# The modulation stage of a hybrid attention and Fourier layer: order of loads, the split of one matrix product between TensorE and VectorE, and the first tile's rows

## The chip, the cores and the metric

The kernel runs on one core of one Trainium2 chip. The metric is the device time of one launch in microseconds (us). Each comparison runs the kernels on the same chip.

## The reference

One layer of a diffusion backbone, in float32, for 256 context tokens (`x_prompt`) and 2048 latent tokens (`x_sample`), 1024 channels. Both streams share all weights.

```
m = silu(cvec) @ w_mod + b_mod              # cvec: c for latent, c_ctx for context tokens; w_mod 1024 x 6144
sh1, sc1, g1, sh2, sc2, g2 = split(m, 6)
h = rms_norm(x, norm1_g) * (1 + sc1) + sh1
q, k, v, f = split(h @ w_in)                # 1024 x 2048: four groups of 512 columns
mix = concat(diff_attention(q, k, v), fourier(f)) @ w_out
x = x + g1 * mix
h = rms_norm(x, norm2_g) * (1 + sc2) + sh2
x = x + g2 * (relu(h @ w1) ** 2 @ w2)
```

The change concerns the way from the inputs to the first rows of `h` and of `h @ w_in`. For these, columns 0 to 2047 of `w_mod` (the shift `sh1` and the scale `sc1`, for both condition vectors) are needed first.

## The kernel before

The tokens are 18 tiles of 128 rows; tiles 0 and 1 are context. The kernel has stages: modulation and projection of all tiles (to about 450 us), Fourier mixing, attention, output projection, MLP. Products with large matrices are made in three passes (`mm3`, L87 to L90): each operand is split into a high half in a shortened float format (`h`, a cast) and the low half that remains (`l`, a subtraction), and high by high, high by low and low by high are summed in PSUM. ScalarE makes the high half, VectorE the low half.

The part at hand (L437 to L549) stands in a `manual_schedule` block: each engine's queue has the order in which the code is written. The loop over tiles 1 to 16 behind it (L552 ff.) is ordered by the scheduler of the framework, which places each instruction by a timeline of its own from the start of the program on; the last tile and the later stages are written out by hand again. Inputs are loaded through SP's queue (`nc.sync`), some small ones through ACT's (`nc.scalar`) and POOL's (`nc.gpsimd`).

In order, the part at hand does this:

- `setup_small` (L92) loads the condition vectors, `b_mod` and the norm gains as rows of one tile, applies SiLU to the two vectors (ScalarE's Exp, VectorE's reciprocal), transposes the tile on TensorE and copies it to `cols`: one column per 128 channels.
- `load(0)` loads tile 0, then eight tiles `wm` of W_mod follow (128 rows x 2048 columns, 1 MB each); `load(1)` stands behind the third.
- `norm` (L204) for tile 0: ScalarE squares and sums, VectorE takes the mean, POOL raises to the power -1/2 (`pow_mhalf`, L85), VectorE scales the rows. TensorE then transposes tile 0 (L451).
- Per W_mod tile, TensorE multiplies three blocks of 512 columns by the two condition columns (L455, in float32: each block is two instructions in the trace), and VectorE multiplies and adds the last 512 columns by one condition value per partition, for both conditions (`macc`, L459 and L461). Behind the fifth stands the `norm` of tile 1.
- W_in is loaded in 16 halves of 512 KB (`w_half`, `win`): six at once, each later one as soon as a half before it has been split.
- `mod_cols` (L480): the sums of two rows are copied out and transposed into columns (L484); VectorE's 512 sums are reduced over partitions by matmuls with a column of ones (L489). Bias and gains make `modc` and `scale1` (L492, L201, L202). `load_gains` (L111) then issues six small loads on POOL's queue, each broadcasting a row of 64 values to 128 partitions.
- Tile 0's transposed rows are modulated (`h_mod`, four on ScalarE and four on VectorE, L500 and L502), and both 512-column parts are split (L510, L511). Tile 1 is transposed (L515).
- For each of eight row blocks `k` of W_in: four high halves on ScalarE (L523), four low halves on VectorE (L524), and TensorE's twelve matmuls of tile 0 with groups 0 to 3, into four PSUM banks `pj`. In between stand tile 1's modulation (blocks 1 to 4), its split (block 5) and the `norm` of tile 2 (block 6).
- `f_post(0)` empties the bank of group 3 (L402); `proj(1, 0)`, the first projection of tile 1, takes that bank.

Of the kernel before, what the change touches and what calls it, by code (L numbers as in the profile page):

```python
# [37 lines left out]
def f32(ap):  # L38
    return ap.bitcast(F32)


def body(tc, a, out):
    nc = tc.nc
    ctx = ExitStack()
    with ctx:
# [43 lines left out]
            nc.tensor.matmul(ps, lh, rl, start=False, stop=False)  # L89
            nc.tensor.matmul(ps, ll, rh, start=False, stop=last)  # L90

        def setup_small(pool, pps):  # L92
# [3 lines left out]
            nc.sync.dma_start(rows[8:16, :], a["c_ctx"].rearrange("(r p) -> r p", p=P))  # L96
            nc.sync.dma_start(rows[32:80, :], a["b_mod"].rearrange("o (r p) -> (o r) p", p=P))
            nc.scalar.dma_start(rows[80:88, :], a["norm1_g"].rearrange("o (r p) -> (o r) p", p=P))
            nc.scalar.dma_start(rows[88:96, :], a["norm2_g"].rearrange("o (r p) -> (o r) p", p=P))
            nc.scalar.dma_start(rows[96:97, :], a["subln_g"])  # L100
            e = pool.tile([16, P], F32, tag="t2", name="e", bufs=6)
# [67 lines left out]

        FIN = {}  # L170

        def mod_sums(t2, pps, sums, gi):

            z = t2(f"quad{gi}")[:, 0:224]
            nc.gpsimd.memset(z, 0.0)
            nc.gpsimd.tensor_add(z[:, 96:128], ident[:, 0:32], ident[:, 32:64])
            for q in (2, 3):
                nc.gpsimd.tensor_add(z[:, 96:128], z[:, 96:128], ident[:, 32 * q:32 * q + 32])
            FIN[gi] = pm = pps.tile([P, 4, 2, 4], F32, tag="pm", name=f"pm{gi}")
            for q in range(4):  # L180
                nc.tensor.matmul(pm, z[:, 96 - 32 * q:224 - 32 * q], sums[:, :, :, q::4], start=(q == 0), stop=(q == 3))
# [48 lines left out]
        with ExitStack() as c1:  # L230
# [6 lines left out]
            def t2(nm):  # L237
                return p1.tile([P, 512], F32, tag="t2", name=nm, bufs=6)
# [197 lines left out]
            wsrc = a["w_in"][0].rearrange("(k p) n -> p k n", p=P)  # L436
            with tc.manual_schedule():  # L437
                with tc.tile_pool(name="p0r", bufs=3) as rows, tc.tile_pool(name="p0m", bufs=KD - 3, side="right") as more:
                    setup_small(p1, pps)
                    load(0)  # L440
                    wm = []
                    for k in range(KD):
                        wm.append((rows if k < 3 else more).tile([P, 2048], F32, tag="row", name=f"wm{k}"))
                        nc.sync.dma_start(wm[k], wmod[:, k, 0:2048])
                        if k == 2:
                            load(1)
                    norm(p1, X[0], "a0")
                    pr = [pp.tile([P, 512], F32, tag="pj", name=f"pr{gi}", bufs=4) for gi in range(4)]
                    pt0 = [pp.tile([P, 4, P], F32, tag="pt", name=f"pta0_{b}") for b in range(2)]
                    for k in range(KD):  # L450
                        nc.tensor.transpose(pt0[k // 4][:, k % 4, :], X[0][:, k * P:(k + 1) * P], ident)  # L451
                    acc = [t2(f"macc3_{s}") for s in range(2)]
                    for k in range(KD):
                        for gi in range(3):
                            nc.tensor.matmul(pr[gi][0:2, :], cols[:, k:k + 9:8], wm[k][:, gi * 512:gi * 512 + 512], start=(k == 0), stop=(k == KD - 1))  # L455
                        for s in range(2):
                            wk, sc = wm[k][:, 1536:2048], cols[:, 8 * s + k:8 * s + k + 1]
                            if k == 0:
                                nc.vector.tensor_scalar_mul(acc[s], wk, sc)  # L459
                            else:  # L460
                                nc.vector.scalar_tensor_tensor(acc[s], wk, sc, acc[s], op0=ALU.mult, op1=ALU.add)  # L461
# [6 lines left out]
                with tc.tile_pool(name="p0h", bufs=6, reuse_waits="tile") as halves:  # L468
# [4 lines left out]
                        wraw.append(halves.tile([P, 1024], F32, tag="half", name=f"win{k}_{h}"))  # L473
                        nc.sync.dma_start(wraw[n], wsrc[:, k, h * 1024:h * 1024 + 1024])

                    for n in range(6):
                        w_half(n)
                    pm = pps.tile([P, 16, 2], F32, tag="pg", name="pm16")

                    def mod_cols(gi):  # L480
                        r = t2(f"mr{gi}")
                        (nc.vector.tensor_copy if gi == 1 else nc.scalar.copy)(r[0:2, :], pr[gi][0:2, :])
                        for j in range(4):
                            nc.tensor.transpose(pm[:, gi * 4 + j, :], r[0:2, j * P:(j + 1) * P], ident[0:2, 0:2])  # L484

                    mod_cols(0)
                    for s in range(2):
                        for j in range(4):
                            nc.tensor.matmul(pm[:, 12 + j, s:s + 1], acc[s][:, j * P:(j + 1) * P], ones, start=True, stop=True)  # L489
                    mod_cols(2)  # L490
                    mod_cols(1)
                    nc.vector.tensor_add(modc[:, 0:16, :], pm, cols[:, 32:48].unsqueeze(2).to_broadcast([P, 16, 2]))  # L492
# [4 lines left out]
                    def h_mod(dst, pt, k, eng):  # L497
                        sc, sh = scale1[:, k, 1:2], modc[:, k, 1:2]
                        if eng is nc.vector:
                            nc.vector.tensor_scalar(dst, pt[:, k % 4, :], sc, sh, op0=ALU.mult, op1=ALU.add)  # L500
                        else:
                            nc.scalar.activation(dst, pt[:, k % 4, :], AF.Identity, bias=sh, scale=sc)  # L502

                    h0 = [t2(f"hTa0_{b}").rearrange("p (k t) -> p k t", k=4) for b in range(2)]
                    for k in range(4):
                        h_mod(h0[0][:, k, :], pt0[0], k, nc.scalar)
                        h_mod(h0[1][:, k, :], pt0[1], 4 + k, nc.vector)
                    for b in range(2):
                        hi, lo = (x[:, b * 4:b * 4 + 4, :] for x in HH[0])
                        nc.vector.tensor_copy(hi, h0[b])  # L510
                        nc.vector.tensor_sub(lo, h0[b], f32(hi))  # L511
                    X.pop(0)
                    pt1 = [pp.tile([P, 4, P], F32, tag="pt", name=f"pta1_{b}") for b in range(2)]
                    for k in range(KD):
                        nc.tensor.transpose(pt1[k // 4][:, k % 4, :], X[1][:, k * P:(k + 1) * P], ident)  # L515
                    X.pop(1)
                    PJ.update({(0, g): pp.tile([P, 512], F32, tag="pj", name=f"pj0_{g}", bufs=4) for g in (3, 2, 0, 1)})
                    hT = p1.tile([P, KD, P], F32, tag="hT", name="hTa1", bufs=1)
                    load(2)
                    for k in range(KD):  # L520
                        for g in range(4):
                            w = wraw[2 * k + g // 2][:, g % 2 * 512:g % 2 * 512 + 512]
                            nc.scalar.copy(wh[g][k], w)  # L523
                            nc.vector.tensor_sub(wl[g][k], w, f32(wh[g][k]))  # L524
                            if g % 2 and 2 * k + g // 2 + 6 < 16:
                                w_half(2 * k + g // 2 + 6)
                        if 1 <= k < 5:
                            for x in (2 * k - 2, 2 * k - 1):
                                h_mod(hT[:, x, :], pt1[x // 4], x, nc.scalar)
                        if k == 5:  # L530
                            nc.scalar.copy(HH[1][0], hT)
                            nc.vector.tensor_sub(HH[1][1], hT, f32(HH[1][0]))
                        if k == 6:
                            norm(p1, X[2], "a2")
                        for g in range(4):
                            mm3(PJ[0, g], HH[0][0][:, k, :], HH[0][1][:, k, :], wh[g][k], wl[g][k], k == 0, k == KD - 1)
                po = c1.enter_context(tc.tile_pool(name="p1o", bufs=2, reuse_waits="tile"))
                f_post(0)
                vo0 = v_out(0)
# [1530 lines left out]
```

## Time and profile before

| | |
|---|---|
| median of 3 runs | 2885.6 us (2884.66 to 2887.24) |
| the profiled run: its time, its span | 2886.51 us, 2884.7 us |
| granted TensorE clock, mean | 0.998 |
| TensorE (PE) busy | 2847.6 us, 99% |
| VectorE (DVE) busy | 2011.5 us, 70% |
| ScalarE (ACT) busy | 1547.0 us, 54% |
| GpSimd (POOL) busy | 1061.7 us, 37% |
| DMA | 492.93 MB, mean 171 GB/s |

A timeline row has start, duration, engine, line, operation, output and inputs, the count of instructions merged into it and, in brackets, how long the engine was idle before it and what released it. The length of a matmul's row contains its way through the array; one follows the other at shorter distances. Starts and names ending in "q" belong to the issuing queue. A row of busy time by stretch has the stretch, its length, the busy time of PE, PEld (weight loads), DVE, ACT and POOL with the number of instructions, the granted TensorE clock, the share of the DMA engines' time, and GB/s.

### The profile page before, as it was taken

How to read it: one execution, taken by the hardware profiler on the slowest of the kernel's cores; microseconds unless marked ns; L12 is line 12 of the kernel's file. 1: busy time of each engine (PE TensorE's matmuls, PEld its weight loads, DVE VectorE, ACT ScalarE, POOL GpSimd, SP SyncE). 2: the span in 40 equal slices, each digit the busy share in tenths (PEclk: the TensorE clock that was granted, in tenths of full speed). 3: DMA queues.
4: the chain of work that ended last, by engine and by line, in shares of the span. 5: the costliest groups of instructions: out<-in, count | busy, mean ns of one | idle time of the engine just before them, and what ended most of it. 6: DMA issues, size and time to landing. Idle time of an engine off the chain costs nothing.

```text
span 2884.7 us, 43207 instructions
## 1 busy us (share of the span) xinstructions
PE 2847.6 (99%) x15119; PEld 2468.6 (86%) x15119; DVE 2011.5 (70%) x3375; ACT 1547.0 (54%) x3503; POOL 1061.7 (37%) x869
## 2 busy tenths in 40 slices
PE   8999999999999999999999999999999999999999
PEld 4888787688888888888889999999998888888887
DVE  6676776898988989865477777778775353345554
ACT  4333322798998989853356565556554332232221
POOL 1112112699999999942223333333332000000000
PEclk9999999999999999999999999999999999999999
DMA  7777888521211312037777677667747464345663
GB/s 283 202 201 190 227 210 231 195 106 43 73 69 45 114 38 98 21 112 208 236 219 233 219 247 229 220 218 238 232 166 254 146 201 137 133 143 185 200 206 110
DMA packets 392779, 492.93 MB, mean 171 GB/s; under 512 B 26467, under 2 KB 306384, under 8 KB 389490
## 3 DMA queue, kind: packets, MB, share of 16 engines
q1 hardware_dynamic: 387136, 479.73, 52.7%
q0 software_dynamic: 1872, 7.28, 0.7%
q10 hardware_dynamic: 3554, 3.17, 0.4%
q8 instruction: 119, 1.95, 0.3%
q14 instruction: 98, 0.80, 0.1%
HBM read 312.58 MB, written 179.59 MB: 171 GB/s over the span
## 4 chain that ended last, share of the span: by engine, by line
PE 91%; DVE 3%; ACT 3%; DMA 2%; issue 1%; POOL 0%; SPq 0%; ACTq 0%; DVEq 0%; POOLq 0%
PE Ss L1022 10%; PE ps L88 8%; PE ps L89 8%; PE ps L90 8%; PE pts L1077 5%; PE po L90 4%; PE po L88 4%; PE po L89 4%; PE pj L88 4%; PE pj L89 4%; PE pj L90 4%; PE pA L1685 2%; PE pA L1686 2%; PE pB L1685 2%; PE pB L1686 2%; PE pB L1687 2%
## 5 line engine op out<-in xcount | busy, mean ns | idle before, releaser
L1027 DVE TENSOR_REDUCE mxs<-Ss 128x1 f32<-128x512 f32 x636 | 413.3, 685 | 63.1 <-PE Ss L1022 52.0
L1362 DVE TENSOR_TENSOR sl<-sr,sh 128x768 fp32r<-128x768 f32 x168 | 161.7, 964 | 337.8 <-ACT sh L1361 337.3
L1062 POOL TENSOR_TENSOR P0s<-P0s,P1s 128x1024 f32<-128x1024 f32 (+2 forms) x128 | 378.7, 2958 | 10.7
L1361 ACT CAST sh<-sr 128x768 fp32r<-128x768 f32 x168 | 140.2, 836 | 424.8 <-PE ps L89 424.8
L1727 POOL TENSOR_TENSOR gs<-g,g 128x384 f32<-128x384 f32 x48 | 69.6, 1451 | 469.8 <-ACT g L1697 410.8
L1046 ACT ACTIVATE P1s<-Ss,mxs 128x512 f32<-128x512 f32 x318 | 215.2, 694 | 36.1 <-DVE mxs L1030 36.1
L88 PE MATMUL pj<-wh,hh 128*128 128x512 f32 x576 | 229.4, 398 | 3.9 <-DVE qn L289 3.2
L89 PE MATMUL ps<-tlT,sh 128*128 128x512 f32 x585 | 229.3, 392 | 0.0
L88 PE MATMUL ps<-thT,sh 128*128 128x512 f32 x585 | 229.0, 391 | 0.0
L89 PE MATMUL pj<-wl,hh 128*128 128x512 f32 x576 | 228.5, 397 | 0.5 <-DVE wl L524 0.5
L90 PE MATMUL ps<-thT,sl 128*128 128x512 f32 x585 | 227.7, 389 | 0.0
L90 PE MATMUL pj<-wh,hl 128*128 128x512 f32 x576 | 227.3, 395 | 0.0
L1046 ACT ACTIVATE P0s<-Ss,mxs 128x512 f32<-128x512 f32 x318 | 214.1, 691 | 5.5 <-DVE mxs L1030 4.9
L1022 PE MATMUL Ss<-KS1s,Qs 128*128 128x512 f32 x636 | 196.2, 420 | 6.2 <-ACT P0s L1046 3.5
L1022 PE MATMUL Ss<-KS0s,Qs 128*128 128x512 f32 x636 | 195.5, 420 | 2.4 <-ACT P1s L1046 2.4
L1077 PEld LDWEIGHTS pts<-ident,P0s 128*128 128x128 f32 x1280 | 157.7, 140 | 42.8 <-issue 2.1
L1077 PE MATMUL pts<-ident,P0s 128*128 128x128 f32 x1280 | 190.5, 272 | 0.7 <-ACT P1s L1046 0.7
L1696 ACT ACTIVATE g<-uz 128x384 f32<-128x384 f32 x144 | 75.8, 527 | 201.0 <-DVE uz L1719 171.3
L1061 POOL TENSOR_SCALAR P1s<-P1s,tots 128x1024 f32<-128x1024 f32 (+2 forms) x128 | 171.7, 1342 | 5.8
L1089 DVE TENSOR_TENSOR als<-pts,ahs 128x512 fp32r<-128x512 f32 x256 | 165.9, 681 | 6.8 <-ACT ahs L1084 6.6
L88 PE MATMUL ps<-ophT,sh 128*128 128x512 f32 x423 | 165.7, 392 | 1.1 <-DVE uz L1719 1.1
L90 PE MATMUL ps<-ophT,sl 128*128 128x512 f32 x423 | 165.7, 392 | 0.0
(531 smaller groups left out, 8056.3 us busy)
## 6 DMA issues: line engine op xcount, KB each, us to landing
sr<-sd SPq DMA_DIRECT2D x84, 768.0 KB
a<-in_w SPq DMA_DIRECT2D x184, 256.0 KB
sd<-gs SPq DMA_DIRECT2D x192, 192.0 KB
sd<-g SPq DMA_DIRECT2D x144, 192.0 KB
wm<-in_w_mod SPq DMA_DIRECT2D x32, 512.0 KB
Qs<-qd SPq DMA_DIRECT2D x32, 512.0 KB
b<-in_w SPq DMA_DIRECT2D x64, 256.0 KB
b<-tsum SPq DMA_DIRECT2D x64, 256.0 KB
```

Source lines behind the costliest of these rows:

```text
L88: nc.tensor.matmul(ps, lh, rh, start=first, stop=False)
L89: nc.tensor.matmul(ps, lh, rl, start=False, stop=False)
L90: nc.tensor.matmul(ps, ll, rh, start=False, stop=last)
L1022: nc.tensor.matmul(S[:, :w], self.Q[:, x, m, j * P:j * P + P], self.hd.KS[m][:, b * 512:b * 512 + w], start=(x == 0), stop=(x == 1))
L1027: nc.vector.tensor_reduce(self.mx[j][:, m, b:b + 1], self.S[j, m, b], axis=AX.X, op=ALU.max)
L1046: nc.scalar.activation(dst, S, AF.Exp, bias=self.mx[j][:, m, 6:7], accum_out=self.sm[j][:, m, b:b + 1])
L1061: nc.gpsimd.tensor_scalar(p, p, tot[:, 3:4], 0.0, op0=ALU.mult, op1=ALU.add)
L1062: nc.gpsimd.tensor_add(d, d, p)
L1077: nc.tensor.transpose(pt[:, c:c + P], self.p0[j][:, (kb + t) * P:(kb + t + 1) * P], ident)
L1089: nc.vector.tensor_sub(t, self.pt[kb], f32(self.A[kb][0]))
L1361: nc.scalar.copy(hi, src)
L1362: nc.vector.tensor_sub(lo, src, f32(hi))
```

## The change

`setup_small` becomes `load_cond`, which only issues the small loads (`c_ctx` now on ACT's queue, `norm1_g` on SP's), and `setup_cond`, which computes and comes after the loads of W_mod. Tile 0 is loaded behind the second W_mod tile, tile 1 behind the second half of W_in, tile 2 (`load(2)`) in row block 1.

VectorE sums 768 of the 2048 columns, TensorE 1280 (512 + 512 + 256). VectorE's sums are reduced by a transposing reduction and four small products with the matrix `quad`, as later modulation groups do. Tile 0's norm stands behind the third W_mod tile, its transposes in pairs behind the fourth to seventh.

The four high halves of row block 0 stand ahead of the scales on ScalarE, the first low half ahead of them on VectorE. Tile 0's rows are made in two parts: channels 0 to 511 (two activations each on ScalarE and VectorE) ahead of the row blocks, the others behind the splits of block 1, where tile 1's norm now stands too. Tile 1's transposes stand behind TensorE's blocks 2 and 4, its modulation in blocks 3 to 6, its split in block 7. Block 7's matmuls go through the groups in the order 3, 2, 0, 1.

```
+        def load_cond(pool):
             rows = pool.tile([P, P], F32, tag="t2", name="rows", bufs=6)
...
-            nc.sync.dma_start(rows[8:16, :], a["c_ctx"]...)
+            nc.scalar.dma_start(rows[8:16, :], a["c_ctx"]...)
-            nc.scalar.dma_start(rows[80:88, :], a["norm1_g"]...)
+            nc.sync.dma_start(rows[80:88, :], a["norm1_g"]...)
...
-                    setup_small(p1, pps)
-                    load(0)
+                    rw = load_cond(p1)
...
-                        if k == 2:
-                            load(1)
-                    norm(p1, X[0], "a0")
+                        if k == 1:
+                            load(0)
+                    setup_cond(p1, pps, rw)
+                    z = quads(t2, "quad0")
+                    pr = [pp.tile([P, 512], F32, tag="pj", name=f"pr{gi}", bufs=4) for gi in range(3)]
...
+                    def at0(k):
+                        return pt0[k // 2 % 2][:, k // 4 * 2 + k % 2, :]
...
                     for k in range(KD):
-                        for gi in range(3):
+                        for gi, w in enumerate((512, 512, 256)):
...
-                            wk, sc = wm[k][:, 1536:2048], ...
+                            wk, sc = wm[k][:, 1280:2048], ...
...
-                        if k == 4:
-                            norm(p1, X[1], "a1")
+                        if k == 2:
+                            norm(p1, X[0], "a0")
+                        if 3 <= k < 7:
+                            for x in (2 * k - 6, 2 * k - 5):
+                                nc.tensor.transpose(at0(x), X[0][:, x * P:(x + 1) * P], ident)
...
+                    def w_high(k, g):
+                        nc.scalar.copy(wh[g][k], w_raw(k, g))
+
+                    def w_rest(k, g):
+                        nc.vector.tensor_sub(wl[g][k], w_raw(k, g), f32(wh[g][k]))
+                        if g % 2 and 2 * k + g // 2 + 6 < 16:
+                            w_half(2 * k + g // 2 + 6)
+
                     for n in range(6):
                         w_half(n)
+                        if n == 1:
+                            load(1)
...
+                    for s in range(2):
+                        nc.vector.tensor_reduce(sums[:, s, :], acc[s]..., axis=AX.X, op=ALU.add, apply_transpose=True)
+                    for gi in range(3):
...
+                        nc.scalar.copy(r[0:2, :w], pr[gi][0:2, :w])
+                        for j in range(w // P):
                             nc.tensor.transpose(pm[:, gi * 4 + j, :], r[0:2, j * P:(j + 1) * P], ident[0:2, 0:2])
...
+                    for q in range(4):
+                        nc.tensor.matmul(pq, z[:, 96 - 32 * q:224 - 32 * q], sums[:, :, q::4], start=(q == 0), stop=(q == 3))
+                    for g in range(4):
+                        w_high(0, g)
+                    w_rest(0, 0)
...
+                    def h_first(b):
+                        for k in range(4 * b, 4 * b + 4):
...
+                            if k in (2, 3):
+                                nc.vector.tensor_scalar(dst, at0(k), sc, sh, op0=ALU.mult, op1=ALU.add)
+                            else:
+                                nc.scalar.activation(dst, at0(k), AF.Identity, bias=sh, scale=sc)
                         hi, lo = (x[:, b * 4:b * 4 + 4, :] for x in HH[0])
...
+                    h_first(0)
...
                     for k in range(KD):
                         for g in range(4):
+                            if k:
+                                w_high(k, g)
+                            if k or g:
+                                w_rest(k, g)
+                        if k == 1:
+                            h_first(1)
+                            norm(p1, X[1], "a1")
+                            load(2)
+                        if 3 <= k < 7:
+                            for x in (2 * k - 6, 2 * k - 5):
+                                nc.scalar.activation(hT[:, x, :], pt1[x // 4]..., AF.Identity, ...)
...
+                        if k == 7:
                             nc.scalar.copy(HH[1][0], hT)
...
-                        for g in range(4):
+                        for g in (3, 2, 0, 1) if k == KD - 1 else range(4):
                             mm3(PJ[0, g], HH[0][0][:, k, :], HH[0][1][:, k, :], wh[g][k], wl[g][k], k == 0, k == KD - 1)
+                        if k in (2, 4):
+                            b = k // 2 - 1
+                            pt1[b] = pp.tile([P, 4, P], F32, tag="pt", name=f"pta1_{b}")
+                            for x in range(4):
+                                nc.tensor.transpose(pt1[b][:, x, :], X[1]..., ident)
```

More of the change, by code (lines that the diff above doesn't have):

```diff
@@ L170, in body, with quads @@
         FIN = {}
-        def mod_sums(t2, pps, sums, gi):
-            z = t2(f"quad{gi}")[:, 0:224]
+        def quads(t2, nm):
+            z = t2(nm)[:, 0:224]
             nc.gpsimd.memset(z, 0.0)
@@ L178, in mod_sums @@
                 nc.gpsimd.tensor_add(z[:, 96:128], z[:, 96:128], ident[:, 32 * q:32 * q + 32])
+            return z
+        def mod_sums(t2, pps, sums, gi):
+            z = quads(t2, f"quad{gi}")
             FIN[gi] = pm = pps.tile([P, 4, 2, 4], F32, tag="pm", name=f"pm{gi}")
@@ L444, in body @@
                         nc.sync.dma_start(wm[k], wmod[:, k, 0:2048])
-                        if k == 2:
-                            load(1)
-                    norm(p1, X[0], "a0")
-                    pr = [pp.tile([P, 512], F32, tag="pj", name=f"pr{gi}", bufs=4) for gi in range(4)]
+                        if k == 1:
[3 more added lines that the diff above has]
+                    pr = [pp.tile([P, 512], F32, tag="pj", name=f"pr{gi}", bufs=4) for gi in range(3)]
                     pt0 = [pp.tile([P, 4, P], F32, tag="pt", name=f"pta0_{b}") for b in range(2)]
+                    def at0(k):
+                        return pt0[k // 2 % 2][:, k // 4 * 2 + k % 2, :]
+                    acc = [f32(p1.tile([P, KD, P], F32R, tag=f"h{x}", name=f"macc_{x}")).rearrange("p k t -> p (k t)")[:, 0:768] for x in "hl"]
                     for k in range(KD):
-                        nc.tensor.transpose(pt0[k // 4][:, k % 4, :], X[0][:, k * P:(k + 1) * P], ident)
-                    acc = [t2(f"macc3_{s}") for s in range(2)]
-                    for k in range(KD):
-                        for gi in range(3):
-                            nc.tensor.matmul(pr[gi][0:2, :], cols[:, k:k + 9:8], wm[k][:, gi * 512:gi * 512 + 512], start=(k == 0), stop=(k == KD - 1))
+                        for gi, w in enumerate((512, 512, 256)):
+                            nc.tensor.matmul(pr[gi][0:2, :w], cols[:, k:k + 9:8], wm[k][:, gi * 512:gi * 512 + w], start=(k == 0), stop=(k == KD - 1))
                         for s in range(2):
-                            wk, sc = wm[k][:, 1536:2048], cols[:, 8 * s + k:8 * s + k + 1]
+                            wk, sc = wm[k][:, 1280:2048], cols[:, 8 * s + k:8 * s + k + 1]
                             if k == 0:
@@ L487, in body @@
[L487 to L492, printed above, removed]
+                    for q in range(4):
+                        nc.tensor.matmul(pq, z[:, 96 - 32 * q:224 - 32 * q], sums[:, :, q::4], start=(q == 0), stop=(q == 3))
@@ L493, in body @@
+                    for g in range(4):
+                        w_high(0, g)
+                    w_rest(0, 0)
+                    nc.vector.tensor_add(modc[:, 0:10, :], pm, cols[:, 32:42].unsqueeze(2).to_broadcast([P, 10, 2]))
+                    nc.vector.tensor_add(modc[:, 10:16, :], pq.rearrange("p s j -> p j s"), cols[:, 42:48].unsqueeze(2).to_broadcast([P, 6, 2]))
                     mk_scale(scale1, 8, 80)
@@ L518, in body @@
                     hT = p1.tile([P, KD, P], F32, tag="hT", name="hTa1", bufs=1)
-                    load(2)
+                    pt1 = [None] * 2
                     for k in range(KD):
                         for g in range(4):
[L522 to L530, printed above, removed]
+                            if k:
[8 more added lines that the diff above has]
+                            for x in (2 * k - 6, 2 * k - 5):
+                                nc.scalar.activation(hT[:, x, :], pt1[x // 4][:, x % 4, :], AF.Identity, bias=modc[:, x, 1:2], scale=scale1[:, x, 1:2])
+                        if k == 6:
+                            norm(p1, X[2], "a2")
+                        if k == 7:
```

42 lines of the change are left out of this document (17 added, 25 removed).

## The prediction

> **What bounds the kernel now.** I read the page's head first, then busy time by stretch, then each engine's timeline through the first 66 us.
>
> ```profile
> span 2884.7 us, 43207 instructions
> 0.00:36.20 36.20, 26.93 (x85) 8.59 (x85) 15.58 (x32) 5.05 (x9) 5.34 (x14) 1.00 0.93 350
> 36.20:66.50 30.30, 27.29 (x113) 21.41 (x113) 25.87 (x44) 26.78 (x57) 0.56 (x1) 0.89 0.62 219
> 66.50:440.00 373.50, 370.31 (x1743) 305.54 (x1744) 271.72 (x499) 122.31 (x264) 66.05 (x39) 1.00 0.80 207
> ```
>
> The columns after the length are PE, PEld, DVE, ACT and POOL busy, granted clock, DMA share and GB/s. From 66.5 us on TensorE is busy for 370.31 of 373.50 us, so whatever brings forward the matmuls there brings forward the end. The change lies wholly ahead of that point. The question is when proj(1, 0), the first projection of tile 1, begins, and whether the loop behind it keeps its order.
>
> The first 36 us are the modulation:
>
> ```profile
> 9.02 1.97 PE L451 MATMUL pta<-ident,x 128*128 128x128 f32 x8 [2.07 <-DVE x L212]
> 10.91 21.80 PE L455 MATMUL pr<-wm,cols 128*2 128x512 f32 x48
> ```
>
> ```profile
> 13.76 1.41 DVE L461 SCALAR_TENSOR_TENSOR macc<-wm,cols,macc 128x512 f32<-128x512 f32 x2 [1.07 <-DMA wm<-in_w_mod]
> 17.53 1.42 DVE L461 SCALAR_TENSOR_TENSOR macc<-wm,cols,macc 128x512 f32<-128x512 f32 x2 [2.35 <-DMA wm<-in_w_mod]
> 20.01 1.41 DVE L461 SCALAR_TENSOR_TENSOR macc<-wm,cols,macc 128x512 f32<-128x512 f32 x2 [1.07 <-DMA wm<-in_w_mod]
> ...
> 25.01 1.41 DVE L461 SCALAR_TENSOR_TENSOR macc<-wm,cols,macc 128x512 f32<-128x512 f32 x2 [0.78 <-DMA wm<-in_w_mod]
> 28.35 1.42 DVE L461 SCALAR_TENSOR_TENSOR macc<-wm,cols,macc 128x512 f32<-128x512 f32 x2 [1.93 <-DMA wm<-in_w_mod]
> ...
> 35.55 0.19 DVE L492 TENSOR_TENSOR modc<-pm,cols 128x32 f32<-128x32 f32 x1 [2.98 <-PE pm L484]
> 35.77 0.17 DVE L201 TENSOR_SCALAR scale<-modc 128x16 f32<-128x16 f32 x1
> 35.98 0.17 DVE L202 TENSOR_TENSOR scale<-scale,cols 128x16 f32<-128x16 f32 x1
> ```
>
> VectorE waits for every W_mod tile, so its rows give the landings: one per 2.48 us (17.53 to 20.01), 3.77 us where x1 lies between (13.76 to 17.53, so x1 costs 1.29), the last at 28.35. TensorE transposes tile 0 first, starts on W_mod at 10.91 and then runs on to 32.71: it is behind the loads and is the bound here. The scales are ready at 35.98 + 0.17 = 36.15.
>
> Then tile 0's rows and W's halves:
>
> ```profile
> 36.19 1.50 ACT L502 ACTIVATE hTa<-pta,modc,scale 128x128 f32<-128x128 f32 x4 [2.87 <-DVE scale L202]
> 37.57 4.26 ACT L523 CAST wh<-win 128x512 fp32r<-128x512 f32 x8
> ```
>
> ```profile
> 37.73 0.43 DVE L510 CAST hh<-hTa 128x512 fp32r<-128x512 f32 x1
> 38.19 0.69 DVE L511 TENSOR_TENSOR hl<-hTa,hh 128x512 fp32r<-128x512 f32 x1
> ...
> 39.86 9.82 DVE L524 TENSOR_TENSOR wl<-win,wh 128x512 fp32r<-128x512 f32 x16
> ```
>
> ```profile
> 39.30 0.78 PE L88 MATMUL pj<-wh,hh 128*128 128x512 f32 x1
> ...
> 65.17 0.39 PE L89 MATMUL pj<-wl,hh 128*128 128x512 f32 x1
> 65.39 0.40 PE L90 MATMUL pj<-wh,hl 128*128 128x512 f32 x1
> 66.47 0.51 PE L88 MATMUL pj<-wh,hh 128*128 128x512 f32 x1 [0.69 <-ACT fo L402]
> ```
>
> Tile 0's first matmul starts at 39.30, its last at 65.39 (0.23 apart when warm), and proj(1, 0) at 66.47, after f_post has emptied a bank.
>
> **The change, part by part.** More prices:
>
> ```profile
> 22.07 0.95 POOL L113 DMA_DIRECT2D qg<-in_q_norm_g  x1
> ```
>
> ```profile
> 20.00:26.00 6.00, 6.00 (x15) 1.19 (x14) 4.55 (x8) 0.00 (x0) 4.10 (x7) 1.00 1.01 421
> 26.00:32.00 6.00, 6.00 (x15) 1.19 (x14) 1.95 (x4) 0.57 (x1) 0.00 (x0) 1.00 1.02 246
> ```
>
> ```profile
> L167 DVE TRANSPOSE_TENSOR_REDUCE sums<-macc x12: 668/702/706, 106.8 to 356.3; 128x16 f32<-128x512 f32 x12
> L181 PE MATMUL pm<-sums,quad x8: 221/283/284, 257.8 to 258.5; 128*128 128x32 f32 x8
> ```
>
> ```profile
> 56.90 1.23 DVE L532 TENSOR_TENSOR hl<-hTa,hh 128x1024 fp32r<-128x1024 f32 x1
> ...
> 61.35 0.75 DVE L212 TENSOR_SCALAR x<-x,nrsa 128x1024 f32<-128x1024 f32 x1 [0.75 <-POOL nrsa L85]
> 62.02 2.49 DVE L524 TENSOR_TENSOR wl<-win,wh 128x512 fp32r<-128x512 f32 x4
> ```
>
> *Loads.* x0 goes behind two W_mod tiles and x1 behind all eight: nothing changes for the last W_mod tile by x0, and x1 gives it 1.29 us. c_ctx on ACT's queue and norm1_g on SP's change places among small loads; TensorE then starts on the first W_mod tile (near 7.5, since 13.76 less two landings less x0's 1.29 is 7.5) instead of at 10.91. From there it is paced by the loads: 2.5 blocks of 512 columns per tile instead of 3, at 21.80/24 = 0.91 us each, are 2.3 us against 2.48. The few tenths that c_ctx may gain or lose are therefore not on the path.
>
> A hidden move costs more. The six gain loads stand on POOL's queue behind the power of a norm. Before, that is tile 1's, and they are issued from 22.07 on; in the six us after 26 the DMA engines move 246 GB/s instead of 421, a loss of 175 x 6 = 1.05 MB or 2.5 us. The last W_mod tile bore 3.34 - 2.48 = 0.86 of it (25.01 to 28.35), W_in's halves the rest. After, they stand behind tile 0's power, which follows the third W_mod tile at 13.76 + 2 = 15.8, so they issue near 16.5 and lie wholly inside the W_mod stream. They may cost it 0.86 to 2.5; I take 2.0, nearer the upper end, since all six are inside. Last landing: 28.35 - 1.29 - 0.86 + 2.0 = 28.2.
>
> The Trainium skill ("DMA: Bandwidth & Descriptors", "Queues, rings and completion order") has each DMA engine take turns between its queues packet by packet. By that rule alone the gains would cost only their own bytes, an estimate of some 0.5 us, and the sum below would end 1.5 us earlier; the 246 GB/s speak against it.
>
> *Sums.* TensorE ends at 28.2 + 2.3 = 30.5 (before: 32.71). VectorE's pair on 768 columns costs 1.42 + 2 x 0.27 = 1.96 (0.27 for 256 columns more, from 1.23 against 0.69 for 512): done at 30.15. Two reductions of 0.70 + 0.27, overlapping a little: 31.95. Four products with the quad matrix, eight passes at some 0.1 plus 0.28: 33.1. Meanwhile ScalarE copies the three sums out and splits W's first row block, VectorE takes one low half (0.69); both fit in the wait. The four high halves stand ahead of tile 0's activations on ScalarE's queue and wait for W's first two halves, at 28.2 + 1.29 = 30.8; if those came after 33, the activations and all behind them would wait as long. The quad matrix is made by POOL, busy 5.34 of the first 36.2 us; if it were late, the four products would wait, and it has some 25 us. Two additions and two scale steps at 0.2, of which three follow 33.1: scales at 33.8, against 36.15.
>
> *Tile 0 in two parts.* Two activations on each of ScalarE and VectorE (1.50/4 each), 34.55; high half 0.43; first matmul at 35.1 instead of 39.30.
>
> *The row blocks k.* VectorE now sets the pace (TensorE's half clock of the start, which doubled its matmuls at 39.30 to 0.78, is hidden by that): low half of the rows to 35.7, seven low halves of W at 9.82/16 = 0.61 to 40.05, second half of tile 0 (1.1) and norm a1, which makes VectorE wait 0.75 for POOL and scale for 0.7: 42.65; block 2 by 45.1, TensorE by 45.8, four transposes of tile 1, 46.3. ScalarE waits for them, and block 4's high halves stand behind it. From there TensorE goes 2.75 per block (12 x 0.23): blocks 3 and 4 to 51.8, transposes 52.3. Then ScalarE: two activations 0.75, block 6 (4.26/8 each) 2.1, two activations 0.7, norm a2's square 1.2: 57.05. VectorE: wait and scale 1.45, block 7's 2.45: 60.95. Block 7 now begins with group 3, whose low half comes last; eleven matmuls follow it: 63.6. As group 3's bank is then long emptied, proj(1, 0) follows directly: 63.6 against 66.47, **2.9 us earlier**. load(2) moves behind W halves 6 to 9 on SP's queue, but its norm comes 15 us later. If W's halves 6 to 9 land late, ScalarE waits; a wait of up to 2 us would be taken out of this gain.
>
> The profiled run took 2886.51 us, so it would take 2883.6; the median of the runs, 2885.6, lies 0.9 lower, so I forecast 2882.7. About 0.2%, 5.8 us here, is what a measurement of this kernel can tell from no change.
>
> **The rivals.**
>
> ```profile
> 309.11 0.50 PE L88 MATMUL pj<-wh,hh 128*128 128x512 f32 x1 [2.08 <-DVE qn L289]
> ```
>
> ```profile
> 306.60:309.10 2.50, 0.43 (x2) 0.00 (x0) 0.70 (x2) 0.61 (x1) 1.73 (x1) 1.00 0.98 192
> 310.00:313.40 3.40, 3.40 (x10) 2.65 (x9) 3.40 (x9) 0.00 (x0) 0.00 (x0) 0.50 0.94 222
> ```
>
> A wait of 2.08 us in the loop is followed by 3.4 us at half clock, which cost 1.7 more: 3.8 us for one such wait.
>
> *The clock and the gains take the gain back.* In block 7 TensorE waits from some 57.8 to 61.0 with only a few transposes of tile 2 in it. If that wait halves the clock as at 309 us (1.7), and the gain loads cost their full 2.5, the change is worth 2.9 - 1.7 - 0.5 = 0.7: 2884.9. For it: the row at 309.11 shows that 2.08 us suffice. Against: the transposes may fill a third of the wait. The Trainium skill ("TensorE: Matmul & The Clock Gate", "Why this matters for your kernels") warns only of idle gaps over some 3 us; by that rule the clock would hold and 2882.7 stand, and the measured 2.08 us is the stricter.
>
> *The loop comes out better.* Its order is laid by the scheduler's own timeline, which begins with this stage. If the new order avoids the one wait at 309, another 3.8 go: 2885.6 - 6.7 = 2878.9. For it: the wait is on VectorE, which has room there; against: in steady state the order should fall back to the same.
>
> *The loop comes out worse: slower.* Each new wait of that kind in the 16 tiles of the loop costs 3.8. It decides from 8.7 us of new waits; three of them give 11.4 - 2.9 = +8.5: 2894.1. For it: TensorE idles only 3.2 of 373.5 us in the loop now, so there is little to win and much to lose; against, as above.
>
> **How the numbers follow.** The sum 0.48, its own range 2881.5 to 2885.2 (a gain of 0.4 with halves 2 us late and the gain loads in full, of 4.0 with the gain loads at 0.86); the clock and the gains 0.11; the better loop 0.25; the worse loop 0.16. The first two are within 0.2%: 0.59. For 8 in 10 the range reaches from 2877 into the better loop's times to 2891, leaving out most of the worse loop's 0.16 and the tail of the better one.
>
> **What would show it.** TensorE's W_mod matmuls should start near 7.5 and end near 30.5, the last W_mod wait of VectorE end near 28.2, the gain loads issue near 16.5, the scales be ready near 33.8, the first pj matmul near 35.1, the last wl of block 7 end near 61, proj(1, 0) start near 63.6, and the wait at 309 stand, 2.9 earlier. I am wrong if the last W_mod tile lands past 29.5 or before 27, if ScalarE waits for W's halves, or if busy TensorE time by stretch shows new gaps after 66 us.

## The result: 7.2 us slower, and the profile after

| | before | after |
|---|---|---|
| median on the same chip (13 runs each) | 2885.21 us (2883.74 to 2888.32) | 2892.45 us (2890.35 to 2895.53) |
| ratio after to before, 95% interval | | 1.0023 (1.0015 to 1.0032) |
| profiled run: its time, its span | 2886.51 us, 2884.7 us | 2892.54 us, 2890.4 us |

The forecast was 2882.7 us with a range to 2891.0. In the profile after, the head of the page and busy time by stretch, with the columns of the prediction:

```profile
span 2890.4 us, 43194 instructions
0.00:36.20 36.20, 23.98 (x75) 6.55 (x75) 19.89 (x30) 6.12 (x11) 5.80 (x17) 1.00 0.93 336
36.20:66.50 30.30, 26.44 (x111) 20.55 (x111) 25.20 (x45) 23.61 (x50) 1.12 (x2) 0.89 0.67 233
66.50:440.00 373.50, 371.36 (x1726) 301.04 (x1725) 269.73 (x495) 121.99 (x263) 66.14 (x39) 1.00 0.78 204
```

TensorE is even busier in the last stretch than before (371.36 against 370.31), at full clock, and yet it gets through fewer instructions in it: 1726 against 1743. That is the main reading of this case, and the sum of busy time hides it.

The first stage, on TensorE's, VectorE's and POOL's timelines:

```profile
7.18 11.27 PE L464 MATMUL pr<-wm,cols 128*2 128x512 f32 x24 [0.56 <-DVE cols L112]
...
26.95 2.31 PE L464 MATMUL pr<-wm,cols 128*2 128x512 f32 x6 [2.35 <-DMA wm<-in_w_mod]
...
31.48 2.31 PE L464 MATMUL pr<-wm,cols 128*2 128x512 f32 x6 [1.85 <-DMA wm<-in_w_mod]
...
38.48 0.79 PE L88 MATMUL pj<-wh,hh 128*128 128x512 f32 x1 [1.98 <-DVE hh L536]
```

```profile
21.97 1.02 DVE L470 SCALAR_TENSOR_TENSOR macc_h<-wm,cols,macc_h 128x768 f32<-128x768 f32 x1 [1.16 <-DMA wm<-in_w_mod]
...
27.00 1.02 DVE L470 SCALAR_TENSOR_TENSOR macc_h<-wm,cols,macc_h 128x768 f32<-128x768 f32 x1 [3.08 <-DMA wm<-in_w_mod]
...
31.53 1.02 DVE L470 SCALAR_TENSOR_TENSOR macc_h<-wm,cols,macc_h 128x768 f32<-128x768 f32 x1 [2.58 <-DMA wm<-in_w_mod]
...
36.95 0.18 DVE L209 TENSOR_TENSOR scale<-scale,cols 128x16 f32<-128x16 f32 x1
```

```profile
16.25 0.96 POOL L116 DMA_DIRECT2D qg<-in_q_norm_g  x1
...
18.81 1.06 POOL L119 DMA_DIRECT2D lq<-in_lambda_k  x2
```

TensorE starts at 7.18 and the gain loads issue from 16.25, as forecast. But behind them the last W_mod tiles land 5.03 and 4.53 us apart instead of 2.48, the last at 31.53 instead of 28.2. Everything behind keeps its forecast distance and is late by this: scales at 37.13, first pj matmul at 38.48. The row blocks end so on TensorE:

```profile
62.31 1.09 PE L228 MATMUL pta<-ident,x 128*128 128x128 f32 x8 [0.79 <-DVE x L219]
...
64.72 0.50 PE L89 MATMUL pj<-wl,hh 128*128 128x512 f32 x1 [1.08 <-DVE wl L496]
...
67.39 0.39 PE L88 MATMUL pj<-wh,hh 128*128 128x512 f32 x1
```

proj(1, 0) starts at 67.39, 0.9 later than before (66.47), not 2.9 earlier. The other 6 us come later, and not as waits. The table of TensorE's waits from 66.5 to 470 us (total, times, longest), before and then after:

```profile
PE pj L88 <- DVE qn L289: 3.2, 3, 2.1
PE pj L88 <- ACT fo L402: 0.7, 1, 0.7
```

```profile
PE pj L88 <- DVE qn L296: 2.0, 2, 1.3
```

`qn` is a tile of VectorE whose lateness holds back the next matmul. The waits have become fewer. What has changed is the distance between matmuls that wait for nothing. The same 71 pj matmuls, from the first to the last start, on the timeline of before and then of after:

```profile
126.22 0.40 PE L89 MATMUL pj<-wl,hh 128*128 128x512 f32 x1
...
142.25 0.40 PE L90 MATMUL pj<-wh,hl 128*128 128x512 f32 x1
```

```profile
128.34 0.39 PE L89 MATMUL pj<-wl,hh 128*128 128x512 f32 x1
...
144.68 0.40 PE L90 MATMUL pj<-wh,hl 128*128 128x512 f32 x1
```

16.03 us for 70 distances are 0.2290 each, 16.34 are 0.2334. The mean over all such distances of the projection is 0.2291 and 0.2333: 4.2 ns more. From 66.5 to 269 us there are 813 pj matmuls, so 3.4 us; the same matmul is late by 0.9 at 66.47 and by 4.3 at 269. To 471 us they are 1601, so 6.7; against this stand 1.2 us fewer waits for qn and the 1.7 of the half clock at 310, which after does not have: 0.9 + 6.7 - 2.9 = 4.7, measured 4.6. A stretch of half clock in the attention (568.6 to 572.1, granted 0.51 there) brings it to some 6; the spans end 5.7 apart.

What differs for these matmuls is where their stationary rows `hh` and `hl` lie (the operand of 128*128 in the timeline's rows; the one of 128x512, from W, is called the moving one). A tag names the place that tiles share in a pool, and the places follow each other in the order in which tags are first opened. The change opens the tags of `hh` and `hl` for VectorE's sums (`macc`), ahead of the four tags `nsq`, `nss`, `nrs` and `ff` that came before them until then. So `hh` lies at byte 39712 of each partition instead of 50080, and `hl` 8192 further up in both. W's tiles, the moving operand, keep their places.

### The profile page after: what moved, and what is told of

Its sections match the earlier page's. It is cut to its first block, busy times and chain, and to the rows that moved or that the text cites. A ratio compares the mean times of both kernels' runs of the same rounds, so it can differ in the third digit from the quotient of the medians.

```text
span 2890.4 us, 43194 instructions
## 1 busy us (share of the span) xinstructions
PE 2851.1 (99%) x15109; PEld 2464.9 (85%) x15109; DVE 2016.5 (70%) x3375; ACT 1549.2 (54%) x3506; POOL 1062.4 (37%) x873
## 4 chain that ended last, share of the span: by engine, by line
PE 87%; DVE 3%; ACT 3%; DMA 2%; POOL 1%; issue 1%; SPq 0%; ACTq 0%; DVEq 0%; POOLq 0%
PE Ss L1055 10%; PE ps L88 8%; PE ps L89 8%; PE ps L90 8%; PE pts L1110 5%; PE po L90 4%; PE po L88 4%; PE po L89 4%; PE pj L88 3%; PE pj L89 3%; PE pj L90 3%; PE pC L1720 2%; PE pB L1720 2%; PE pB L1718 2%; PE pB L1719 2%; PE pC L1718 2%
```

## The experiments

Each experiment's `before` is that kernel on the same chip, 2884.4 to 2885.0 us.

**Only the addresses, in the kernel before.**

```
                     load(0)
+                    for x in "hl":
+                        p1.tile([P, KD, P], F32R, tag=f"h{x}", name=f"first_{x}")
```

> The kernel before, with one thing changed: the tags of tile rows hh and hl are opened ahead of the small norm tiles, so hh and hl begin at byte 39712 of each partition instead of 50080 (modulo 512: 288 instead of 416), as in the kernel after. No instruction is added, removed or moved. Address theory: the distance of two pj matmuls in the projection goes from 0.229 to 0.233 us; over some 1650 of them that is 7 us: 2892 us. Rival (the slower pace of the kernel after comes from the edited stage or from the order of the loop that the scheduler lays): pace 0.229, 2885 us.

Measured: 2891.29 us, ratio 1.0024 (1.0014 to 1.0034), distance 0.2333. Apart from a few semaphore waits, all four compute engines carry the same instructions in the same order as before; the addresses alone cost 6.3 us.

**The changed kernel with the old addresses**: the four tags are opened ahead of `macc`.

```
+                    p1.tile([P, D], mybir.dt.bfloat16, tag="nsq", name="first_sq", bufs=1)
+                    for x in ("nss", "nrs"):
+                        p1.tile([P, 1], F32, tag=x, name=f"first_{x}")
+                    p1.tile([P, 512], F32, tag="ff", name="first_ff", bufs=4)
                     acc = [...tag=f"h{x}", name=f"macc_{x}"...]
```

> The kernel after, with hh and hl put back to byte 50080 by opening the tags of the norm tiles and of ff first. Address theory: pace back to 0.229, 7 us faster than the kernel after: 2885.5 us, about as the kernel before, with the start of proj(1, 0) still near 67.4. Rival: pace stays at 0.233, 2892 us.

Measured: 2886.3 us, ratio 1.0007 (0.9999 to 1.0016), distance 0.2291. That is 1.3 us above before on its chip, where after lies 7.2 above before on its own: 5.9 of the 7.2 are gone.

**The gain loads later**: `load_gains` behind tile 1's norm in row block 1, and then the same with the old addresses.

```
-                    lq = load_gains(p1)
...
                             norm(p1, X[1], "a1")
+                            lq = load_gains(p1)
                             load(2)
```

> The kernel after, with the six gain loads issued behind tile 1's norm in row block 1 instead of ahead of the row blocks, so that they leave the W_mod stream. Theory (the gain loads hold up W_mod): last W_mod tile at 27 instead of 31.5, scales ready near 33, proj(1, 0) near 63.5 instead of 67.4: 4 us faster than the kernel after, 2888.5 us; the pace of pj stays at 0.233. Rival (W_mod's last three tiles are late for another reason, such as the order of the loads on SP's queue): last W_mod tile stays near 31.5, 2892 us.

> The kernel after with both: hh and hl back at byte 50080 and the gain loads behind tile 1's norm. If the two causes are separate and add up: 7 + 4 us faster than the kernel after, 2881 us, 4 below the kernel before. If they are one cause, or the gain is lost to block 7's wait: 2885 us.

Measured: 2889.3 us, ratio 1.0017 (1.0008 to 1.0026), and 2884.87 us, ratio 1.0003 (0.9994 to 1.0012). In the first of them the last W_mod wait ends at 26.28 and the scales are ready at 31.8, 5.3 us earlier than in after. More than half of that is lost again (proj(1, 0) starts near 65.2, 2.2 earlier): now the gain loads meet W_in's later halves. ScalarE's timeline of the first of the two:

```profile
51.35 1.14 ACT L493 CAST wh<-win 128x512 fp32r<-128x512 f32 x2 [3.23 <-DMA win<-in_w_in]
```

So 192 KB in six small loads cost several us in each of the two streams, W_mod and W_in, that somebody waits for. The two changes together did not reach the 2881 of two causes that add up: proj(1, 0) starts only at 66.53 there.

**Is it GpSimd's queue?** The gain loads on ScalarE's queue, behind tile 0's norm (`load_gains` is given the queue).

```
-                    lq = load_gains(p1)
...
                             norm(p1, X[0], "a0")
+                            lq = load_gains(p1, nc.scalar)
```

> The kernel after with the six gain loads issued at the same time, behind tile 0's norm, but on ScalarE's DMA queue instead of GpSimd's. Theory A (small packets of 256 bytes among packets of 8 KB cost the stream, on whichever queue): the W_mod landings stay 5.0 and 4.5 us apart behind the issue, last W_mod matmul near 33.8, first pj matmul near 38.5, time 2892. Theory B (GpSimd's queue or its descriptors cost it): landings 2.5 to 3 apart, last W_mod matmul near 29.5, first pj matmul near 34.5; proj(1, 0) near 64.5 instead of 67.4, time 2889.5.

Measured: 2890.78 us, ratio 1.0024 (1.0015 to 1.0034). VectorE's wait for the last W_mod tile here, and then in the next kernel, where no gain load runs beside W_mod:

```profile
28.18 1.02 DVE L470 SCALAR_TENSOR_TENSOR macc_h<-wm,cols,macc_h 128x768 f32<-128x768 f32 x1 [0.68 <-DMA wm<-in_w_mod]
```

```profile
26.17 1.02 DVE L474 SCALAR_TENSOR_TENSOR macc_h<-wm,cols,macc_h 128x768 f32<-128x768 f32 x1 [0.54 <-DMA wm<-in_w_mod]
```

Without gain loads 26.17, on ScalarE's queue 28.18, on GpSimd's 31.53: they cost W_mod 2.0 or 5.4 us. The view of DMA by queue from 14 to 34 us (packets, MB, share of the 16 engines' time), after and then here:

```profile
q0 software_dynamic: 192, 0.20, 16.4%
```

```profile
q10 hardware_dynamic: 864, 0.20, 4.5%
```

16.4% of 20 us are 3.3 us of all 16 engines for 0.20 MB, which at the 421 GB/s of the stream would be 0.5. Theory B holds for W_mod, but only half for the path: W_in's halves were late as well (ScalarE waited 2.92 us for them, to 34.90), so the first pj matmul came at 37.26, against 38.48 in after and 33.02 in the next kernel. At least a part of this lateness is not the loads' traffic: SP issued the first half of W_in at 25.55 here and at 11.63 in after. SP's queue waited here:

```profile
SPq L488 <- DMA wm<-in_w_mod: 17.2, 2, 15.0
```

In the built program the loads of SP's and ScalarE's queues use eight semaphores in turn, and six more loads among them make the first half of W_in wait for the seventh W_mod tile. The gain loads also issued earlier here, from 11.2 on. So this run shows 2.0 us instead of 5.4 for W_mod, but it does not compare the two queues in this alone.

**The gain loads behind tile 2's norm, old addresses.** In row block 6 W_in has nearly landed.

```
                         if k == 6:
                             norm(p1, X[2], "a2")
+                            lq = load_gains(p1)
```

> The kernel after with hh and hl back at the addresses of before and the six gain loads behind tile 2's norm (row block 6), where W_in has mostly landed. If the gain loads cost only what they collide with: no wait of ScalarE for W_in's halves over 1 us, scales near 31.8, proj(1, 0) near 63.5 to 64.5 (2 to 3 us ahead of before's 66.47), time 2882.5 to 2883.5, faster than before by about 2.5. Rival (the first 66 us don't matter, the loop gives it back): 2885, as with the gain loads behind tile 1's norm.

Measured: 2881.51 us, ratio 0.9992 (0.9983 to 1.0001). First pj matmul at 33.02, proj(1, 0) at 63.74, 2.7 ahead of before. The interval of its time just includes no change. Nor is this gain the forecast one: the forecast's 2.9 us has 2.0 us for the gain loads in it, so without them its sum gives proj(1, 0) at 61.6, and this is 2.1 later. On TensorE block 7 still waits, and here the clock is halved behind this wait, for 3.4 us, which costs some 1.7 (a row of 0.63 instead of 0.39):

```profile
59.51 0.77 PE L89 MATMUL pj<-wl,hh 128*128 128x512 f32 x1 [1.07 <-DVE wl L500]
...
60.50 0.63 PE L88 MATMUL pj<-wh,hh 128*128 128x512 f32 x1
```

**A version that missed**: the last one, `hh` and `hl` 64 bytes further up, tile 2's norm behind block 7, and block 7's splits in the order of its matmuls.

> The last one with three more edits: the unused tile of 64 bytes ahead of hh and hl (address theory: pj matmuls 0.2275 to 0.228 apart, 1 to 2.6 us over the loop), tile 2's norm behind block 7's splits and matmuls instead of ahead of them (VectorE's wait for POOL and its scaling, 1.45 us, leave the path to the last low half), and block 7's splits in the order 3, 2, 0, 1 of its matmuls (the wait of 1.08 us for the last low half goes). Sum: proj(1, 0) near 61.5 to 62.5, time 2878 to 2881. Rival (each is given back): 2884 or more.

Measured: 2886.82 us, ratio 1.0010 (1.0001 to 1.0019). With the norm gone, nothing held the gain loads on POOL's queue: they issued at 39.79, behind tile 1's power, and met W_in's halves:

```profile
52.05 2.39 ACT L498 CAST wh<-win 128x512 fp32r<-128x512 f32 x4 [3.67 <-DMA win<-in_w_in]
```

It is the trap of the change itself: on a queue whose other work is moved, a load moves with it.

**Which addresses are good?** An unused tile ahead of `hh` and `hl` in the kernel before moves them, and group 2's tiles of W, by its size. With 64 bytes:

```
+                    p1.tile([P, 16], F32, tag="pad", name="pad", bufs=1)
                     HH.update({i: tuple(p1.tile(...tag=f"h{x}"...) for x in "hl") for i in range(2)})
```

> The kernel before with one unused tile of 64 bytes per partition opened ahead of hh and hl, so that the stationary rows of the projection lie 64 bytes further up (hh at byte 50144 instead of 50080, residue 480 instead of 416 modulo 512, the residue of the moving W tiles of three groups); W's tiles of group 2 move by 64 as well, to residue 288. Address theory (the distance of two back-to-back pj matmuls depends on the addresses of stationary and moving rows relative to each other; equal residues were the fastest elsewhere in these traces, 0.2275 us): distance 0.2275 to 0.228 instead of 0.229, so some 1 to 2.6 us faster, 2882.5 to 2884. Rival (only the place 39712 is slow, whatever the residue): 0.229 and 2885, no change.

Measured: 2884.63 us, ratio 0.9998 (0.9990 to 1.0007): no difference that the times can tell. The trace shows one, in the table below. With 192 bytes, and with 128 bytes ahead of the early tags of the first experiment:

> The kernel before with an unused tile of 192 bytes ahead of hh and hl: residue 96 instead of 416. A fourth residue for the address theory; no theory says beforehand which distance it gives, 0.2275 to 0.234. If all residues but 288 gave 0.229, 288 would be the special one; if 96 gives another distance again, it is a matter of degree.

> The kernel before with hh and hl opened as early as in the kernel with the early tags, but behind an unused tile of 128 bytes: hh at byte 39840 instead of 39712, so in the low place of the changed kernel, with the residue of before (416 modulo 512 instead of 288). If the residue decides: two pj matmuls 0.229 us apart and 2884 to 2886, no change against before. If the place decides: 0.233 and 2891, as with the early tags alone.

Measured: 2886.9 us in one run, and 2887.69 us, ratio 1.0011 (1.0002 to 1.0020). Neither theory met the second: the distance was 0.2292 for three of W's groups but 0.2330 for group 2, whose tiles had moved. So neither the place nor the residue of `hh` decides, but the two operands' relation. For each kernel, the mean distance of two pj matmuls that follow each other directly, worked out from the starts in its trace (about 1220 distances of groups 0, 1 and 3, 380 of group 2), beside moving address less stationary address, modulo 256. A distance is counted to the group of the earlier matmul of the two; the addresses are those of the built programs:

```
kernel            groups 0, 1, 3       group 2
before            64    0.2291 us      64    0.2291 us
after            192    0.2333        192    0.2333
before + 64        0    0.2280         64    0.2297
before + 192     128    0.2327         64    0.2295
early tags + 128  64    0.2292        192    0.2330
after + 192        0    0.2281        192    0.2333
fastest            0    0.2275          0    0.2285
```

The last two rows were run to test the rule that the first five suggest: 0 is best, 64 costs some 1.5 ns, 128 and 192 cost 5. First the change as it is, with one unused tile:

```
+                    p1.tile([P, 48], F32, tag="pad", name="pad", bufs=1)
                     acc = [...tag=f"h{x}", name=f"macc_{x}"...]
```

> The kernel after, all of the change kept, with one unused tile of 192 bytes ahead of hh and hl: hh at byte 39904 instead of 39712. Rule read from the runs so far (address of the moving tile less that of the stationary, modulo 256): 0 for groups 0, 1 and 3, so 0.2280 us; 192 for group 2, whose tiles move by 192 bytes too, so 0.2333. Against 0.2333 for all in the kernel after this is 1.224 thousand matmuls x 5.3 ns = 6.5 us: 2886. If the low place were slow in itself, or only the residue 416 good, 0.2327 to 0.2333 and 2892.

Measured: 2886.55 us, ratio 1.0005 (0.9997 to 1.0014), 1.6 us above before on its chip, so 5.7 of after's 7.2 are gone, at the distances foretold. The 71 matmuls take 16.06 us:

```profile
127.38 0.39 PE L89 MATMUL pj<-wl,hh 128*128 128x512 f32 x1
...
143.44 0.39 PE L90 MATMUL pj<-wh,hl 128*128 128x512 f32 x1
```

**The versions that beat both.** The gain loads on SP's queue behind W_in's last half, block 7 in its matmuls' order, tile 2's norm behind its splits; old addresses, then 64 bytes up, then group 2 set right too.

```
                         if k == 6:
-                            norm(p1, X[2], "a2")
+                            lq = load_gains(p1, nc.sync)
                         if k == 7:
+                            norm(p1, X[2], "a2")
...
-                        for g in range(4):
+                        for g in (3, 2, 0, 1) if k == KD - 1 else range(4):
                             if k:
                                 w_high(k, g)
```

> The kernel after with hh and hl at the addresses of before; the gain loads on SP's queue behind W_in's last half instead of GpSimd's (in a queue with the halves they can't come between them); block 7's splits in the order 3, 2, 0, 1 of its matmuls; tile 2's norm behind these splits instead of ahead of them. Expected: no wait of ScalarE for W_in over 1 us, no wait of TensorE in block 7 for the last low half (1.08 in the three kernels before it), proj(1, 0) near 62.5, 1.5 to 2 us before that of the kernel whose gain loads stand behind tile 2's norm; time 2879.5 to 2880.5. Rival (TensorE's halved clock at the start or a late tile 2 takes it back): 2882 or more.

> The last one with an unused tile of 64 bytes ahead of hh and hl (residue 480). In the kernel before, this alone made the pj matmuls 0.2282 us apart instead of 0.2291 and the profiled span 1.2 us shorter. Expected 1 to 1.5 us less than the last one: 2878 to 2879.5; the same if the 0.0009 us is lost in the loop's waits.

> The fastest kernel so far (hh and hl 64 bytes up, gain loads behind W_in on SP's queue, block 7's order) with a second unused tile of 192 bytes behind hh and hl, so that group 2's tiles come to the distance 0 modulo 256 too. By the rule all four groups at 0.2280 instead of 0.2298 for group 2: 0.7 us less, 2877, which the times can hardly tell and the distances in the trace can. Without the rule: group 2 anywhere between 0.2275 and 0.2335.

Measured: 2878.11 us, ratio 0.9980 (0.9972 to 0.9989); 2877.57 us, ratio 0.9977 (0.9967 to 0.9986); 2877.47 us, ratio 0.9974 (0.9963 to 0.9984). The last one on TensorE's timeline: first pj matmul, the remainder of block 7's wait, proj(1, 0), and the 71 matmuls, in 15.91 us:

```profile
33.20 0.79 PE L88 MATMUL pj<-wh,hh 128*128 128x512 f32 x1 [1.98 <-DVE hh L541]
...
56.71 0.51 PE L89 MATMUL pj<-wl,hh 128*128 128x512 f32 x1 [0.20 <-DVE wl L502]
...
60.02 0.50 PE L88 MATMUL pj<-wh,hh 128*128 128x512 f32 x1 [0.53 <-ACT fo L409]
...
120.47 0.40 PE L89 MATMUL pj<-wl,hh 128*128 128x512 f32 x1
...
136.38 0.39 PE L90 MATMUL pj<-wh,hl 128*128 128x512 f32 x1
```

proj(1, 0) is 6.4 ahead of before. The three differ by less than their runs scatter; only the distances (0.2291, 0.2279 with 0.2298 for group 2, 0.2277 over all groups) set them apart. What each of the three edits gives alone was not run. The nearest pair is the version that missed and the second of these, which differ in the place of the gain loads and of tile 2's norm: 1.8 us above before and 6.8 below, with proj(1, 0) at 63.08 and 58.73. Their waits for qn came to 3.5, 3.2 and 3.6 us, against 2.0 in after: a part of the faster pace is waited away again.

## Why the prediction was wrong

*The step that failed* is its argument on the bound: "whatever brings forward the matmuls there brings forward the end", and behind it "The change lies wholly ahead of that point". It took the loop's own pace as fixed, and none of the rivals gave a moved buffer a price. But the change also moved two buffers that the loop reads. The distance rose by 4.2 ns on 1601 matmuls, 6.7 us; the addresses alone, in the kernel before, make 6.3 us, and taking them back in after gives 5.9. The diff said it: `macc` is opened with the tags of `hh` and `hl`, ahead of tags that used to come first.

*The second miss* is the size of one term: the gain loads. Taken at 2.0 us between 0.86 and 2.5, they cost W_mod 5.4 (31.53 against 26.17, and the 26.2 that the prediction's sum has without them). The 2.5 was read from the six us in which before's stream was seen to slow, which begin 4 us behind the first of these loads. In after TensorE's wait for W_mod moved proj(1, 0) from a gain of 2.7 (as measured with the loads in row block 6) to a loss of 0.9. The Trainium skill ("DMA: Bandwidth & Descriptors", "Issuing engines are not separate DMA queues") says that DMAs started by the scalar, sync or gpsimd engine "will ultimately run on the same 16 DMA engines and interleave with each other, regardless of the engine that started them". The traces agree that the loads come between, but what they took was not the same: 16.4% of the engines' time for 0.20 MB on GpSimd's queue, 4.5% on ScalarE's, at different moments.

*What held.* TensorE's start (7.18 for 7.5), the issue of the gain loads (16.25 for 16.5), the scales 5.6 us behind the last landing (33.8 less 28.2; 37.13 less 31.53), the first pj matmul 1.3 behind them, 28.9 us for the row blocks (28.5 forecast). ScalarE waited for W's halves only 0.75 us. There were no new gaps after 66 us.

*The rivals.* The half clock in block 7 did not come in after, where the wait was 1.08 us; in the kernel with the late gain loads it came behind 1.07. "The loop comes out better" came in part: the wait of 2.08 at 309 us shrank to 1.29 without a half clock, and with the other waits that gave 2.9 of the 3.8. "The loop comes out worse" put its number, 2894.1, near the result by luck: it counted new waits, and those did not come.

*What stays open*: why the distance depends on the operands' addresses; whether the half clock in after's attention belongs to the change (the kernel with the gain loads in row block 1 and the one with 128 bytes ahead of the early tags have one there too, before has none; the mean granted clock of single runs goes from 0.997 to 0.999 both before and after, so such stretches change from run to run, and a profile shows one run); and the total cost of the gain loads on either queue at the same moment.

## What to carry to other kernels

When a diff opens a buffer earlier than before, list which tiles move, and compare the start-to-start distance of untouched matmuls, not their busy time: a few ns on 1600 of them outweighed a whole stage here. In this kernel small broadcast loads did best on the queue of the large stream, behind it, where they cannot come between; on another queue they move with whatever work stands ahead of them there.

## What was unexpected of the hardware

At the full granted clock the next matmul starts 0.2275 to 0.2333 us after a 128x512 pj matmul, by that matmul's moving address less its stationary address modulo 256 (0 best, 128 and 192 worst, steps of 64 tried), foretold right for two kernels. Two later stages agree, whose addresses the change leaves alone: in before the `ps` matmuls with 0.2274 at 0, 0.2292 at 64 and 0.2333 at 192, the `po` matmuls on W_out with 0.2266 at 0 and 0.2316 at 128. In `po` the two values take turns, so there it shows to which matmul a distance belongs: counted to the later one, it would be 0.2327 at 0 and 0.2304 at 128.

A wait of 1.07 us was followed by half clock in one kernel and one of 1.08 was not in another, so the length of a wait by itself did not decide. In all sixteen traces the changes of the granted clock lie whole multiples of 3.41 us apart. In the step of 3.41 us that holds the wait, TensorE was busy for 1.45 us in the first of the two kernels (56.15 to 59.56) and for 2.33 in the other (63.47 to 66.88). That would fit a decision by the busy time of a step, but no clean threshold comes out: a step with 1.49 us kept its clock (560.96 to 564.37 in the version that missed), and one with 1.65 did not (52.19 to 55.61 with the gain loads in row block 1 and the old addresses).
